# Chunk totals of the log-decays taken from the sum over later tokens and transposed; an odd tile's gate rows taken from the operands of products 3 and 7

## The chip, the cores and the metric

The kernel runs on one core of a Trainium2 chip. The metric is the device time of one execution in microseconds (us), the median of several runs. Engines are named as in the profile: PE is TensorE's matmul pipe (PEld its weight loads), DVE is VectorE, ACT is ScalarE, POOL is GpSimd, SP is SyncE, whose work here is to issue DMAs.

## The reference, cut to what matters

One block of a model: a gated linear attention mixer, then a convolutional feed-forward, each with an RMS norm before it and a residual behind it, and a last norm. The sequence has 2048 tokens, the model 1024 channels, the mixer 4 heads with 128 key and 256 value channels, in chunks of 64 tokens. Only the gate path is touched:

```python
proj = h @ w_in
q, k, v, r, glr = jnp.split(proj, [hk, 2 * hk, 2 * hk + hv, 2 * hk + 2 * hv], axis=-1)   # glr: 16 columns
log_a = jax.nn.log_sigmoid((glr @ w_gate2 + b_gate).astype(jnp.float32)) / GLA_TAU
g = jnp.cumsum(lac, axis=2)            # inside each chunk of 64 tokens
g_end = g[:, :, -1]
k_dec = kc * jnp.exp(g_end[:, :, None] - g)
# per chunk: state = state * exp(g_end) + k_dec^T v;  o = q state
```

So each token needs the exponential of the sum of the log-decays of the tokens that come later in its chunk (it scales the token's key), and each chunk needs the exponential of the whole sum (it scales the state). For the last token of a chunk the first of the two is exp(0) = 1.

## The kernel before, in words

The 2048 tokens are 16 tiles of 128 tokens, two chunks to a tile. The mixer's projections run in four passes over eight pairs of tiles: R (the gate r, and the 16 columns glr), A and B (keys, queries and values of two heads each, with the scan over chunks woven in) and Y (the output projection); the feed-forward follows. Each pass multiplies a pair of tiles (even and odd) with a 1024x1024 block of weights by a seven-product scheme: the left operands are blocks of the pair and their differences, for the odd tile's halves b12 and b22 for instance p5 = b12 - b11, p7 = b22 - b12 and p3 = b22, and for the even tile p1 = b11 and p2 = b21. The order of the products is p1, p5, p6, p7, p4, p2, p3 (PORD). Each is 512 wide and is worked in split single precision: a value is a rounded high part and a rest, and three matmuls make one (`mm3p`, lines 177 to 179, which the profile names mp_R, mp_A and so on; an operand's split is lines 186, ACT, and 187, DVE).

Beside the products of pass R, `gate_mm` makes the gate rows glr of both tiles in one PSUM bank pg: 32 weight columns (the 16, once as high part and once as rest), 128 tokens wide, two matmuls for each of four blocks of 128 channels. The even tile takes p1 and p2. The odd tile takes b11 (p1's operand) plus b12 - b11 (p5's) for the upper half of the channels, and p3's for the lower half, so that p1 is multiplied twice, once for each tile. That is 16 matmuls behind p1 and 8 each behind p5, p2 and p3. After p3, `gate_rows` copies pg into gstk, and after every second pair `gates` works on four tiles: a matmul pz, a softplus (ACT, L555), the split of it in lh and ll (`halves`), and then `sums` for each tile.

`sums` multiplies lh and ll by the mask `later` (L566: 128x128, one where the row token is later than the column token in the same chunk) into the bank pd, takes its exponential (L571, ACT) into es, which a DMA stores (L574). The totals of the two chunks come from eight further matmuls (L570) with lh and ll as weights, one head's 128 channels at a time, and a two-column indicator `chunk` as the moving operand; their exponential (L573, ACT) goes to `dec`, one column for each chunk and head. `scan_f` later loads es again (E) and multiplies the keys by it (L646, kd); the state update (L686) multiplies by dec.

The program is written in one order, with a model clock (`adv`) by which work set aside with `later_do` or in `wevents` is called in between the products. From that order a scheduler at build time makes each engine's order by what it expects to be ready, so the order on an engine is not always that of the program. Each engine then works strictly through its own list.

Of the kernel before, what the change touches and what calls it, by code (L numbers as in the profile page):

```python
# [10 lines left out]
F32 = mybir.dt.float32  # L11
F32R = mybir.dt.float32r
BF16 = mybir.dt.bfloat16
AF = mybir.ActivationFunctionType
ALU = mybir.AluOpType

P = 128
# [3 lines left out]
def f32(ap):  # L21
    return ap.bitcast(F32)
# [3 lines left out]
def hybrid_kernel(  # L26
# [17 lines left out]
    nc = tc.nc  # L44
    x = x[0]
    out = out[0]
# [5 lines left out]
    H, DK, DV, RANK = 4, 128, 256, 16  # L52
    CH = 64
    T = 512
    NT = T // P
    NTT = S // P
    NP = NTT // 2
    KT = D // P
    HK = KT // 2
    NF = F // P  # L60
    QSCALE = float(DK) ** -0.5
    ITAU = 1.0 / 16.0
# [5 lines left out]
    SB = 8  # L68
# [25 lines left out]
    cst = ctx.enter_context(tc.tile_pool(name="cst", bufs=1))  # L94
# [29 lines left out]
    def mm_ps(name):  # L124
        return ps.tile([P, 512], F32, tag="mm", name=name, bufs=4)

    def aux_ps(name):
        return ps.tile([P, 512], F32, tag="aux", name=name, bufs=4)
# [20 lines left out]
    def later_do(us, fn):  # L149
        heapq.heappush(delayed, (clock["now"] + us, next(seq), fn))  # L150

    def adv(us):

        clock["now"] += us
        if clock["busy"]:
            return
        clock["busy"] = True
        for due in (wevents, delayed):
            while due and due[0][0] <= clock["now"]:
                heapq.heappop(due)[-1]()  # L160
        clock["busy"] = False
# [22 lines left out]
    def split(hi, lo, src):  # L184

        nc.scalar.copy(hi, src)  # L186
        nc.vector.tensor_sub(lo, src, f32(hi))  # L187


    ident = cst.tile([P, P], F32, name="ident")  # L190
# [4 lines left out]
    halo = cst.tile([P, 2 * NF, 2], F32, name="halo")  # L195
    dec = cst.tile([P, H, S // CH], F32, name="dec")
    nw2 = cst.tile([P, KT], F32, name="nw2")

    def small(tag, name, n=1, kind=""):
        return cst.tile([P, n], F32, tag=tag + kind, name=name, bufs=4)  # L200
# [164 lines left out]
    rp = {}  # L365
# [75 lines left out]

    def masks():
        rp["later"] = rp["p"].tile([P, P], F32R, name="later")
        rp["chunk"] = rp["p"].tile([P, 2], F32R, name="chunk")

        later_f = rp["p"].tile([P, 512], F32, tag="s2k", name="later_f", bufs=SB)
        nc.gpsimd.memset(later_f[:, :P], 1.0)
        nc.gpsimd.affine_select(
            out=later_f[:, :P], in_=later_f[:, :P], compare_op=ALU.is_gt, fill=0.0,
            base=0, pattern=[[-1, P]], channel_multiplier=1,  # L450
        )
        nc.gpsimd.memset(later_f[CH:P, 0:CH], 0.0)
        nc.vector.tensor_copy(rp["later"], later_f[:, :P])


        ind_f = rp["p"].tile([P, 512], F32, tag="s2k", name="ind_f", bufs=SB)
        nc.gpsimd.memset(ind_f[:, :2], 0.0)
        nc.gpsimd.memset(ind_f[0:CH, 0:1], 1.0)
        nc.gpsimd.memset(ind_f[CH:P, 1:2], 1.0)
        nc.vector.tensor_copy(rp["chunk"], ind_f[:, :2])  # L460

    def gate_weights():

        GR = 2 * RANK
        rp["wg"] = wg = rp["p"].tile([P, 2, KT, GR], F32R, name="wg")
        graw = rp["p"].tile([P, 512], F32, tag="s2k", name="graw", bufs=SB)
        gv = graw[:, :KT * RANK].rearrange("p (a b) -> p a b", b=RANK)
        nc.sync.dma_start(gv, wv[:, :, OR + H * DV:OR + H * DV + RANK])
        nc.gpsimd.memset(f32(wg[:, 1, :, RANK:GR]), 0.0)
        nc.vector.tensor_copy(wg[:, 0, :, :RANK], gv)  # L470
        nc.vector.tensor_copy(wg[:, 1, :, :RANK], gv)
        nc.vector.tensor_sub(wg[:, 0, :, RANK:GR], gv, f32(wg[:, 0, :, :RANK]))

    def gate_weights2():

# [33 lines left out]

    def gate_mm(j, o, hh, hl):  # L510

        if o not in ("p1", "p5", "p2", "p3"):
            return
        GR = 2 * RANK
        if o == "p1":
            rp["pg"] = mm_ps(f"pg_{j}")
        pg = rp["pg"]
        wg = rp["wg"]
        k0 = HK if o in ("p2", "p3") else 0
        for c in {"p1": (0, 1), "p5": (1,), "p2": (0,), "p3": (1,)}[o]:  # L520
            out = pg[:GR, c * P:(c + 1) * P]
            kw = {} if o == "p1" and c == 0 else {"skip_group_check": True}
            for k in range(HK):
                ks = slice(k * P, (k + 1) * P)
                nc.tensor.matmul(out, wg[:, 1, k0 + k, :], hl[:, ks], start=(o == "p1" and c == 0 and k == 0), stop=False, **kw)
                nc.tensor.matmul(out, wg[:, 0, k0 + k, :], hh[:, ks], start=False, stop=(k == HK - 1), **kw)
                adv(0.12)
        if o == "p3":
            gate_rows(j)

# [12 lines left out]
    def gates(b, t0, t1, t2):  # L543

        es, L = [], []

        def s2k(name, dt=F32):
            return rp["p"].tile([P, 512], dt, tag="s2k", name=name, bufs=SB)

        def softplus(half):  # L550
            for tt in (2 * half, 2 * half + 1):
                pz = aux_ps(f"pz_{b}_{tt}")
                nc.tensor.matmul(pz, rp["gstk"][0:98, tt * P:(tt + 1) * P], rp["w2s"][0:98, :], start=True, stop=True)
                e = s2k(f"e_{b}_{tt}")
                nc.scalar.activation(e, pz, AF.Softplus, scale=-1.0)  # L555
                es.append(e)

        def halves(tt):
            lh, ll = s2k(f"lh_{b}_{tt}", F32R), s2k(f"ll_{b}_{tt}", F32R)
            split(lh, ll, es[tt])  # L560
            L.append((lh, ll))

        def sums(tt):
            pd = aux_ps(f"pd_{b}_{tt}")
            for i in range(2):
                nc.tensor.matmul(pd, rp["later"], L[tt][1 - i], start=(i == 0), stop=(i == 1))  # L566
            pe = aux_ps(f"pe_{b}_{tt}")
            for h in range(H):
                for i in range(2):
                    nc.tensor.matmul(pe[:, 2 * h:2 * h + 2], L[tt][1 - i][:, h * DK:(h + 1) * DK], rp["chunk"], start=(i == 0), stop=(i == 1))  # L570
            nc.scalar.activation(es[tt], pd, AF.Exp, scale=-ITAU)  # L571
            t = b * NT + tt
            nc.scalar.activation(dec[:, :, 2 * t:2 * t + 2], pe[:, :2 * H].rearrange("p (a b) -> p a b", b=2), AF.Exp, scale=-ITAU)  # L573
            nc.sync.dma_start(ed[t], es[tt])  # L574
            ready.add(f"gates{t}")
            if tt + 1 < NT:
                later_do(0.4 * t2, lambda: halves(tt + 1))

        later_do(t0, lambda: softplus(0))
        later_do(t0 + 2.0, lambda: softplus(1))  # L580
        later_do(t0 + 4.0, lambda: halves(0))
        for tt in range(NT):
            later_do(t0 + t1 + t2 * tt, lambda tt=tt: sums(tt))
# [51 lines left out]
    def scan_f(n):  # L635
        if n not in scan:
            return
        g, t, kq, e = (scan[n][k] for k in ("g", "t", "kq", "e"))
        if sp.get("gnw_of") != g:
            sp["gnw_of"] = g  # L640
            sp["gnw"] = sp["a"].tile([P, 512], F32, tag="gnw", name=f"gnw_{g}", bufs=1)
            nc.sync.dma_start(sp["gnw"], gla_norm_w[512 * g:512 * (g + 1)].partition_broadcast(P))
        kz = sp["kz"]
        q = sp["q"][t % 2]
        kd = sp["a"].tile([P, 2 * DK], F32, tag="kd", name=f"kd_{n}", bufs=1)
        nc.vector.tensor_mul(kd, kq[:, :2 * DK], e)  # L646
        for c in range(2):
            own = slice(c * CH, (c + 1) * CH)
            split(kz[0][own, c, :], kz[1][own, c, :], kd[own, :])
        pq = aux_ps(f"pq_{n}")  # L650
        for h in range(2):
            nc.tensor.transpose(pq[:, h * P:(h + 1) * P], kq[:, (2 + h) * DK:(3 + h) * DK], ident)
        pv = pq[:, :2 * P].rearrange("p (a c s) -> p a c s", c=2, s=CH)
        for c in range(2):
            sl = (slice(None), slice(None), slice(2 * c * CH, (2 * c + 1) * CH))
            nc.scalar.activation(q[0][sl], pv[:, :, c, :], AF.Copy, scale=QSCALE)
            nc.vector.scalar_tensor_tensor(q[1][sl], pv[:, :, c, :], QSCALE, f32(q[0][sl]), op0=ALU.mult, op1=ALU.subtract)
        r = scan[n]["r"] = sp["a"].tile([P, 512], F32, tag="r", name=f"r_{n}", bufs=2)
        nc.sync.dma_start(r, rd[t][g])
        nc.scalar.activation(r, r, AF.Silu)  # L660
        nc.gpsimd.tensor_mul(r, r, sp["gnw"])
# [230 lines left out]
    def first_pair():  # L892
# [24 lines left out]
        for t in range(2):  # L917
            norm_x(t)
            blocks_x(t)
        masks()  # L920
        nc.gpsimd.memset(halo, 0.0)
        b = {}
# [575 lines left out]
    for n, (o, s) in enumerate(units):  # L1498
# [10 lines left out]
        for q in range(NQ):  # L1509
            k = n * NQ + q  # L1510
# [43 lines left out]
```

## Time and profile before

| | |
|---|---|
| median of 3 runs | 2225.44 us (2217.04 to 2226.3) |
| profiled execution | 2224.22 us, span 2222.5 us |
| PE busy | 2122.4 us, 95% of the span, 9952 matmuls |
| DVE, ACT, POOL busy | 1636.5, 1107.9, 733.1 us |
| granted TensorE clock, mean | 0.986 of full speed |

The span is what the profiler saw from the first to the last instruction; the profiled execution's own time is 1.7 us longer. Busy shares are means over stages that are limited by different things, so a change in pass R (about 53 to 241 us) is read from rows of that stretch.

### The profile page before, as it was taken

Reading aid. Unit: us, or ns where it says so; the run is one execution under the profiler, and the core shown is the slowest. Engines: PE = TensorE matmul, PEld = TensorE weight load, DVE = VectorE, ACT = ScalarE, POOL = GpSimd, SP = SyncE. Lnnn points to the kernel's source line nnn. Section 1 sums busy time; section 2 is a strip of 40 time slices with the busy share of each in tenths; the row PEclk is TensorE's granted clock in tenths of the full one; section 3 lists DMA queues with packets and bytes.
Section 4 is the critical chain, followed back from the end, with each engine's and each line's share of the span. In section 5 each row is a group of like instructions: output and inputs, shape, how many; then the busy total and the mean of one; then the engine's idle time right before and its main releaser. Section 6 shows DMA issues by size and latency. Waiting matters only on the chain.

```text
span 2222.5 us, 29090 instructions
## 1 busy us (share of the span) xinstructions
PE 2122.4 (95%) x9952; PEld 1743.6 (78%) x9952; DVE 1636.5 (74%) x2167; ACT 1107.9 (50%) x2024; POOL 733.1 (33%) x602
## 2 busy tenths in 40 slices
PE   6999999989998999898999999999999999999998
PEld 5888787877887787677887777788888887888886
DVE  8655787789778765488899786897877777457564
ACT  5554755565556676444555453454554443333342
POOL 1000011111111000355566664656555435036100
PEclk9999999999999999999999999999999999999999
DMA  6645684478557889935435348433332468354453
GB/s 210 218 165 182 203 264 157 131 223 299 164 161 235 283 321 352 315 117 174 155 120 193 105 139 288 142 112 102 103 111 85 159 243 289 128 180 152 142 176 113
DMA packets 305125, 411.78 MB, mean 185 GB/s; under 512 B 23742, under 2 KB 160110, under 8 KB 304976
## 3 DMA queue, kind: packets, MB, share of 16 engines
q1 hardware_dynamic: 267440, 346.99, 47.2%
q10 hardware_dynamic: 37536, 62.93, 8.4%
q8 instruction: 78, 1.28, 0.2%
q14 instruction: 71, 0.58, 0.1%
HBM read 266.70 MB, written 143.13 MB: 184 GB/s over the span
## 4 chain that ended last, share of the span: by engine, by line
PE 62%; DVE 14%; DMA 9%; issue 7%; ACT 3%; POOL 3%; SPq 1%; ACTq 0%; DVEq 0%; POOLq 0%
PE ua L177 5%; PE pd_p L178 5%; PE pd_p L179 5%; PE pd_p L177 5%; PE ua L179 5%; PE ua L178 5%; DVE t L1237 4%; PE uc L177 2%; PE uc L179 2%; PE uc L178 2%; PE mp_R L177 2%; PE mp_R L179 2%; PE mp_R L178 2%; PE mp_Y L177 2%; PE mp_Y L179 2%
## 5 line engine op out<-in xcount | busy, mean ns | idle before, releaser
L177 PE MATMUL ua<-h_p,uw_p 128*128 128x512 f32 x704 | 280.2, 398 | 23.6 <-ACT c L1219 23.6
L178 PE MATMUL ua<-h_p,uw_p 128*128 128x512 f32 x704 | 278.6, 396 | 0.0
L179 PE MATMUL ua<-h_p,uw_p 128*128 128x512 f32 x704 | 278.4, 395 | 0.0
L1237 DVE SCALAR_TENSOR_TENSOR t<-u,cw,t 128x1024 f32<-128x1024 f32 x176 | 263.3, 1500 | 8.9 <-ACT t L1235 7.9
L178 PE MATMUL pd_p<-dw_p,da 128*128 128x512 f32 x616 | 240.5, 390 | 3.1 <-DVE da L187 3.1
L179 PE MATMUL pd_p<-dw_p,da 128*128 128x512 f32 x616 | 240.1, 390 | 0.0
L177 PE MATMUL pd_p<-dw_p,da 128*128 128x512 f32 x616 | 240.1, 390 | 0.0
L187 DVE TENSOR_TENSOR uw_p<-ur,uw_p 128x512 fp32r<-128x512 f32 x176 | 168.3, 972 | 58.5 <-ACT uw_p L186 53.3
L187 DVE TENSOR_TENSOR da<-da_p,da 128x512 fp32r<-128x512 f32 x154 | 133.6, 920 | 105.4 <-ACT da L186 105.3
L186 ACT CAST da<-da_p 128x512 fp32r<-128x512 f32 x154 | 85.2, 619 | 208.9 <-PE pd_p L179 153.3
L177 PEld LDWEIGHTS ua<-h_p,uw_p 128*128 128x128 f32 x704 | 134.1, 191 | 57.2 <-ACT c L1219 27.6
L186 ACT CAST uw_p<-us 128x512 fp32r<-128x512 f32 x132 | 82.1, 622 | 165.8 <-POOL us L1199 108.3
L187 DVE TENSOR_TENSOR uw_p<-us,uw_p 128x512 fp32r<-128x512 f32 x132 | 120.4, 921 | 57.6 <-ACT uw_p L186 57.2
L179 PEld LDWEIGHTS ua<-h_p,uw_p 128*128 128x128 f32 x704 | 134.0, 190 | 30.1
L178 PEld LDWEIGHTS ua<-h_p,uw_p 128*128 128x128 f32 x704 | 134.3, 191 | 29.5
L177 PE MATMUL uc<-h_p,uw_p 128*128 128x512 f32 x352 | 138.3, 393 | 1.0 <-DVE t L1237 1.0
L179 PE MATMUL uc<-h_p,uw_p 128*128 128x512 f32 x352 | 138.0, 392 | 0.0
L178 PE MATMUL uc<-h_p,uw_p 128*128 128x512 f32 x352 | 138.0, 392 | 0.0
L178 PEld LDWEIGHTS pd_p<-dw_p,da 128*128 128x128 f32 x616 | 116.0, 188 | 28.0 <-DVE da L187 3.9
L1235 ACT ACTIVATE t<-u,cw 128x1024 f32<-128x1024 f32 x88 | 109.8, 1247 | 51.2 <-DVE u L1328 43.3
L179 PEld LDWEIGHTS pd_p<-dw_p,da 128*128 128x128 f32 x616 | 116.0, 188 | 24.2
L177 PEld LDWEIGHTS pd_p<-dw_p,da 128*128 128x128 f32 x616 | 115.9, 188 | 24.0
(269 smaller groups left out, 5476.2 us busy)
## 6 DMA issues: line engine op xcount, KB each, us to landing
ur<-in_ffn_w_up_dram SPq DMA_DIRECT2D x168, 256.0 KB, 3.7
da_p<-ad_p SPq DMA_DIRECT2D x154, 256.0 KB, 4.1
h_p<-hd_p SPq DMA_DIRECT2D x56, 512.0 KB, 8.1
ad_p<-as_p SPq DMA_DIRECT2D x88, 256.0 KB, 2.7
ad_p<-t SPq DMA_DIRECT2D x66, 256.0 KB, 3.5
x<-in_x_dram SPq DMA_DIRECT2D x32, 512.0 KB, 4.3
ch<-in_ffn_w_down_dram SPq DMA_DIRECT2D x61, 256.0 KB, 4.4
hr_A_p<-h1d_p SPq DMA_DIRECT2D x56, 256.0 KB, 2.7
```

The lines of the kernel that those rows point to most:

```text
L177: nc.tensor.matmul(ps_ap, ah, bl, start=(first and i == 0), stop=False, **kw)
L178: nc.tensor.matmul(ps_ap, al, bh, start=False, stop=False, **kw)
L179: nc.tensor.matmul(ps_ap, ah, bh, start=False, stop=(last and i == len(pairs) - 1), **kw)
L186: nc.scalar.copy(hi, src)
L187: nc.vector.tensor_sub(lo, src, f32(hi))
L1235: nc.scalar.activation(t, u[:, 2:2 + TS], AF.Identity, scale=cw[:, 2, c:c + 1], bias=cw[:, 3, c:c + 1])
L1237: nc.vector.scalar_tensor_tensor(t, u[:, k:k + TS], cw[:, k, c:c + 1], t, op0=ALU.mult, op1=ALU.add)
```

## The change

Two things are changed. In `sums` the mask `later` gets a column of ones over the own chunk for the last token of each chunk, so that rows 63 and 127 of pd hold the chunk totals in place of zero; es is then transposed on PE, head by head, and DVE copies columns 63 and 127 of the result to dec. The eight narrow matmuls, the mask `chunk` and the second exponential go. Since the keys' factor of a chunk's last token must stay 1, `scan_f` takes the maximum of E and `lastrow` (1 in rows 63 and 127, 0 elsewhere) in the same instruction that multiplies the keys. In `gate_mm` the odd tile's gate rows come from p7 = b22 - b12, with the upper half's weights negated, and p3 = b22, with the sum of both halves' weights; the new weights wgx are made once, by DVE and POOL, from work set aside in `gate_weights`. p1 is multiplied once, p5 no longer.

```diff
 def masks():
-        rp["chunk"] = rp["p"].tile([P, 2], F32R, name="chunk")
...
+        nc.gpsimd.memset(later_f[0:CH, CH - 1:CH], 1.0)
+        nc.gpsimd.memset(later_f[CH:P, P - 1:P], 1.0)
         nc.vector.tensor_copy(rp["later"], later_f[:, :P])
-        ind_f = rp["p"].tile([P, 512], F32, tag="s2k", name="ind_f", bufs=SB)
-        nc.gpsimd.memset(ind_f[:, :2], 0.0)
-        nc.gpsimd.memset(ind_f[0:CH, 0:1], 1.0)
-        nc.gpsimd.memset(ind_f[CH:P, 1:2], 1.0)
-        nc.vector.tensor_copy(rp["chunk"], ind_f[:, :2])
+        nc.vector.tensor_add(lastrow, ident[:, CH - 1:CH], ident[:, P - 1:P])
 def gate_weights():
+        rp["wgx"] = wgx = rp["p"].tile([P, 2, KT, GR], F32R, name="wgx")
...
+        nc.gpsimd.memset(f32(wgx[:, 1, :, RANK:GR]), 0.0)
+        def others():
+            gx_ = graw[:, KT * RANK:2 * KT * RANK].rearrange("p (a b) -> p a b", b=RANK)
+            nc.vector.tensor_add(gx_[:, :HK], gv[:, :HK], gv[:, HK:])
+            nc.vector.tensor_scalar(gx_[:, HK:], gv[:, :HK], -1.0, 0.0, op0=ALU.mult, op1=ALU.add)
+            nc.vector.tensor_copy(wgx[:, 0, :, :RANK], gx_)
+            nc.vector.tensor_copy(wgx[:, 1, :, :RANK], gx_)
+            nc.vector.tensor_sub(wgx[:, 0, :, RANK:GR], gx_, f32(wgx[:, 0, :, :RANK]))
+        later_do(24.0, others)
 def gate_mm(j, o, hh, hl):
-        if o not in ("p1", "p5", "p2", "p3"):
+        if o not in ("p1", "p2", "p3", "p7"):
...
-        k0 = HK if o in ("p2", "p3") else 0
-        for c in {"p1": (0, 1), "p5": (1,), "p2": (0,), "p3": (1,)}[o]:
+        c = int(o in ("p3", "p7"))
+        wg = rp["wgx" if c else "wg"]
+        k0 = HK if o in ("p2", "p7") else 0
 def sums(tt):
             for i in range(2):
                 nc.tensor.matmul(pd, rp["later"], L[tt][1 - i], start=(i == 0), stop=(i == 1))
+            nc.scalar.activation(es[tt], pd, AF.Exp, scale=-ITAU)
+            t = b * NT + tt
             pe = aux_ps(f"pe_{b}_{tt}")
             for h in range(H):
-                for i in range(2):
-                    nc.tensor.matmul(pe[:, 2 * h:2 * h + 2], L[tt][1 - i][:, h * DK:(h + 1) * DK], rp["chunk"], start=(i == 0), stop=(i == 1))
-            nc.scalar.activation(es[tt], pd, AF.Exp, scale=-ITAU)
-            t = b * NT + tt
-            nc.scalar.activation(dec[:, :, 2 * t:2 * t + 2], pe[:, :2 * H].rearrange("p (a b) -> p a b", b=2), AF.Exp, scale=-ITAU)
+                nc.tensor.transpose(pe[:, h * DK:(h + 1) * DK], es[tt][:, h * DK:(h + 1) * DK], ident)
+            pv = pe.rearrange("p (h c s) -> p h c s", c=2, s=CH)
+            nc.vector.tensor_copy(dec[:, :, 2 * t:2 * t + 2], pv[:, :, :, CH - 1])
             nc.sync.dma_start(ed[t], es[tt])
 def scan_f(n):
-        nc.vector.tensor_mul(kd, kq[:, :2 * DK], e)
+        nc.vector.scalar_tensor_tensor(kd, e, lastrow, kq[:, :2 * DK], op0=ALU.max, op1=ALU.mult)
```

## Rows read from the trace of the kernel before

**Rows 1.** Stretches: us, PE, PEld, DVE, ACT, POOL busy (instructions), PE clock, DMA share, GB/s.

```profile
50.00:80.00 30.00, 29.93 (x169) 24.46 (x168) 26.02 (x40) 13.97 (x26) 3.52 (x4) 1.00 0.83 291
80.00:110.00 30.00, 29.98 (x180) 24.88 (x179) 17.14 (x27) 18.03 (x33) 1.41 (x2) 1.00 0.47 159
...
290.00:520.00 230.00, 216.78 (x1138) 182.39 (x1137) 190.56 (x351) 131.56 (x299) 33.26 (x33) 0.98 0.62 200
```

**Rows 2.** Waits of PE, 50 to 280 us and whole span: total us, times, longest.

```profile
PE mp_A L177 <- ACT cp_A L1128: 3.9, 1, 3.9
PE mp_R L178 <- DVE h_R_p L187: 0.8, 1, 0.8
...
PE px L718 <- DVE og L710: 8.5, 6, 3.7
```

**Rows 3.** The chain that ended last, pieces between 92 and 111 us: start, us, what.

```profile
93.06 0.87 PE pt_a L397 x8
93.94 0.47 PE pd L566 x2
94.40 0.34 PE mp_R L177
94.74 0.23 PE mp_R L178
...
96.59 0.79 PE pe L570 x8
...
106.97 0.06 PE pg L525
...
107.45 0.28 PE mp_R L177
```

**Rows 4.** DVE and PE instructions by line: ns min/median/max, first and last start.

```profile
L718 PE MATMUL px<-ident,og x128: 270/272/473, 297.6 to 744.6; 128*128 128x128 f32 x128
L472 DVE TENSOR_TENSOR wg<-graw,wg x1: 279/279/279, 16.1 to 16.1; 128x128 fp32r<-128x128 f32 x1
L646 DVE TENSOR_TENSOR kd<-o_A,E x16: 415/418/1556, 268.4 to 475.3; 128x256 f32<-128x256 f32 x16
L686 DVE SCALAR_TENSOR_TENSOR state<-state,dec,pk x128: 465/474/482, 282.4 to 736.3; 128x256 f32<-128x256 f32 x128
```

**Rows 5.** The timeline of ACT around the exponentials of pd: start, us, instruction.

```profile
95.03 0.60 ACT L571 ACTIVATE e<-pd 128x512 f32<-128x512 f32 x1
...
105.42 0.60 ACT L571 ACTIVATE e<-pd 128x512 f32<-128x512 f32 x1 [1.96 <-PE pd L566]
...
268.97 1.28 ACT L571 ACT_TABLE_LOAD   x1
270.27 0.60 ACT L571 ACTIVATE e<-pd 128x512 f32<-128x512 f32 x1
...
275.04 0.60 ACT L571 ACTIVATE e<-pd 128x512 f32<-128x512 f32 x1
```

**Rows 6.** The timeline of PE: the second matmul of pd for the same four tiles.

```profile
94.01 0.40 PE L566 MATMUL pd<-lh,later 128*128 128x512 f32 x1
...
104.99 0.39 PE L566 MATMUL pd<-lh,later 128*128 128x512 f32 x1
...
267.33 0.39 PE L566 MATMUL pd<-lh,later 128*128 128x512 f32 x1
...
274.61 0.39 PE L566 MATMUL pd<-lh,later 128*128 128x512 f32 x1
```

**Rows 7.** The timeline of PE at the first state update of the scan.

```profile
280.24 0.39 PE L680 MATMUL pk<-vl,kz 128*128 128x256 f32 x1 [0.26 <-POOL kz L616]
280.46 0.40 PE L177 MATMUL mp_A<-w_A_p,h_A_p 128*128 128x512 f32 x1
```

**Rows 8.** The timeline of PE after the longest wait at the start of pass A.

```profile
254.57 0.53 PE L177 MATMUL mp_A<-w_A_p,h_A_p 128*128 128x512 f32 x1 [3.86 <-ACT cp_A L1128]
254.91 0.62 PE L178 MATMUL mp_A<-w_A_p,h_A_p 128*128 128x512 f32 x1
```

More of the change, by code (lines that the diff above doesn't have):

```diff
@@ L197, in hybrid_kernel @@
     nw2 = cst.tile([P, KT], F32, name="nw2")
+    lastrow = cst.tile([P, 1], F32, name="lastrow")
     def small(tag, name, n=1, kind=""):
@@ L516, in gate_mm @@
             rp["pg"] = mm_ps(f"pg_{j}")
-        pg = rp["pg"]
-        wg = rp["wg"]
-        k0 = HK if o in ("p2", "p3") else 0
-        for c in {"p1": (0, 1), "p5": (1,), "p2": (0,), "p3": (1,)}[o]:
[L521 to L527, printed above, removed]
+        c = int(o in ("p3", "p7"))
+        wg = rp["wgx" if c else "wg"]
+        k0 = HK if o in ("p2", "p7") else 0
+        out = rp["pg"][:GR, c * P:(c + 1) * P]
+        kw = {} if o == "p1" else {"skip_group_check": True}
+        for k in range(HK):
+            ks = slice(k * P, (k + 1) * P)
+            nc.tensor.matmul(out, wg[:, 1, k0 + k, :], hl[:, ks], start=(o == "p1" and k == 0), stop=False, **kw)
+            nc.tensor.matmul(out, wg[:, 0, k0 + k, :], hh[:, ks], start=False, stop=(k == HK - 1), **kw)
+            adv(0.12)
         if o == "p3":
```

## The prediction

> **What bounds the kernel now.** I read the stretches first. In pass R PE is busy for all but 0.1 us of every 30, while DVE and ACT have 4 to 16 us to spare [rows 1]. The granted clock is 1.00, the upper level of 2.4 GHz. The waits of PE between 50 and 280 us agree: two entries, one of 3.9 us at the start of pass A, one of 0.8 [rows 2]. The chain that ended last, read next, runs on PE through pass R. So from about 53 to 241 us each microsecond taken off PE's list is one off the time, and each one added is one more. At the end of R and in A the chain passes to weight loads, DVE and ACT, but all of that is released by PE's progress in R and moves with it. In A PE works 216.8 of 230 us and DVE 190.6 [rows 1]: there a wait counts in part only.
>
> PE's real price of an instruction is its start to start in the chain, not its busy time, because matmuls overlap. A main product costs 0.23 us. A group of eight chunk-total matmuls costs 0.79 us, a pair of pd 0.47, eight transposes of x 0.87, one gate matmul 0.06. The first product behind narrow work starts dearer: 0.34 in place of 0.23 behind pd, 0.28 behind gate matmuls [rows 3].
>
> **The gate rows.** Seven pairs go through `gate_mm` (the first pair takes `gate_plain`, untouched). Each has 40 matmuls now and 32 afterwards. The number of blocks stays four (p1, p7, p2, p3 for p1, p5, p2, p3), so the dearer first product behind a block is paid as often as now. What goes is 7 x 8 x 0.06 = **-3.4 us** [rows 3]. I see no reason for less or more.
>
> The block behind p5 moves behind p7, two products later. So p5's operand pair comes free 0.5 us earlier and p7's 0.5 us later, and with it ACT's cast for a later operand. PE has waited for such an operand once, for 0.8 us [rows 2], so I take nothing; with that cover gone it would be 7 x 0.5 = 3.4 us. No DMA is added or moved; on SP's queue the store of es has the same place and the same releaser, the exponential.
>
> **The new weights.** Five small DVE instructions of at most 0.28 us each [rows 4], 1.4 us in all, called at 24 us of the model clock, which by the order of the code is the start of the second pair, near 55 us. They are wanted at its p7, some 10 us later. DVE is busy 26.0 of 30 us there and PE does not wait [rows 1, 2]: nothing, or 1.4 us once if they hold up an operand that PE wants. POOL's memsets fall where it is nearly idle (3.5 of 30 us busy [rows 1]): nothing.
>
> **The chunk totals.** Sixteen times, eight narrow matmuls (0.79 us) give way to four transposes. By the transposes of x these cost 0.87 / 2 = 0.44 us [rows 3]: 16 x 0.35 = -5.6 us. But the narrow matmuls mostly stand right behind pd now, so that the dearer next product (0.34 for 0.23) is paid once for both. The transposes wait for the exponential, so products will stand between pd and them, and the 0.11 is paid twice: up to 16 x 0.11 = +1.8 us, about +1.5 since two of the sixteen groups, the one at 96.59 for instance, are apart already [rows 3]. Sum **-4.1 us**.
>
> The Trainium skill speaks against this trade: "TensorE: Matmul & The Clock Gate", Part 4 on PE-mode transpose, gives about 275 ns for one 128x128 transpose in a kernel's context. The busy time of one here is indeed 272 ns [rows 4], but the row of the chain has eight of them in 0.87 us. By the page's figure, taken as start to start, four would be an estimated 1.10 us and the whole trade would lose time; that case is a rival below.
>
> **The new wait.** This is the unknown. Before, the narrow matmuls needed only lh and ll. Now PE needs es, which ACT makes after pd, and every product queued behind the transposes on PE waits with them. From the end of pd's second matmul to the end of the exponential it is 105.42 + 0.60 - 104.99 - 0.39 = 0.64 us where ACT is free, 1.22 us with a table load in front (95.63 - 94.41), and 3.15 us at worst (270.87 - 267.72) [rows 5, 6]. I did this for all 16 tiles (first and last are shown): 22.7 us, of which seven tiles have 0.63 to 0.70 and nine have 1.22 to 3.15, together 18.1.
>
> How much of it PE pays depends on where the transposes stand in its list. That list is not the program's: pk's first matmul is followed by a main product [rows 7], though the program issues pk's six in a row, and at 94.40 nine main products stand between pd and the narrow matmuls that follow it in the code [rows 3]. So the scheduler fills with products (0.23 us each) what it expects to wait. Below: it expects each exponential rightly, and PE pays nothing. Above: it fills 0.66 us for every tile and never expects a table load or a late ACT; the nine long tiles then cost 18.1 - 9 x 0.66 = 12.2 us. Directly behind pd, without filling, would be the full 22.7; that is a rival. Between the ends I go by the nearest row, PE transposes that wait for a value of another engine: px for og, 8.5 us over 128 / 4 = 32 groups, 0.27 us each [rows 2, 4]. Sixteen of them: **+4.3 us**.
>
> What else hangs on it: ACT loses 16 short exponentials and DVE gets 16 copies of eight elements, on engines with room in R [rows 1]. Were a copy late, its bank of the four `aux` ones would come free late; dec itself is wanted only by the scan, after 280 us. Nothing. The masks come before the first sums by some 70 us. Nothing.
>
> **The keys' factor.** 32 instructions of DVE change kind. The median of the multiply is 418 ns, that of the state update, of the new kind and the same size though from PSUM, 474 ns [rows 4]: +0.06 us each, 1.8 us on DVE in A and B. PE does not wait for kd directly there, and DVE is not full; between 0 and 1.8, I take **+0.5 us**.
>
> **Sum.** -3.4 - 4.1 + 4.3 + 0.5 = -2.7 us. The profiled execution took 2224.2 us (span 2222.5 and 1.7 around it), 1.2 us under the median of the three runs. 2224.2 - 2.7 = **2221.5 us**. With the wait at 0 and at 12.2 it is 2217.2 and 2229.4, the likeliest case's own range. I can tell a change from none at about 0.5%, 11 us.
>
> **Rivals.**
>
> *All hidden.* The scheduler places the transposes well and PE pays under 0.1 us a tile: -7.0 us, 2217. For it: PE hardly waits in R, where everything else was placed by the same scheduler. Against it: px.
>
> *The start of pass A is mended as well.* PE waits 3.86 us there for an ACT copy, and the nine products after it start 0.43 apart at half clock (0.62 us long for 0.39 [rows 8]), 1.8 us more. If the freed ACT time and earlier buffers (lh and ll lose their reader on PE) take this wait away too, then -7.0 - 5.7 = -12.7 us, 2211.5. Against it: ACT is late there for weight casts that the change does not touch.
>
> *The transposes stand right behind pd.* Then PE pays the 22.7 us, no dearer product twice (-9.0 in place of -7.5), and behind the longest stalls the clock goes down to 1.2 GHz as it did after 3.86 us, three times 1.8 us: -9.0 + 22.7 + 5.4 + 0.5 = +19.6 us, 2244, slower than before. It decides from a mean stall of 1.2 us a tile on (16 x 1.2 = 19.2, against 9.0 saved). Against it: the filling seen in [rows 3, 7]. For it: nine of sixteen lags are above 1.2 us, and one product is 0.23.
>
> *The transposes do not overlap.* Four take 4 x 0.27 = 1.09 us: the trade gives 16 x 0.30 + 1.5 = +6.3 in place of -4.1, and the time is 2232. Against it stands the row of eight in 0.87 us [rows 3]. The figure of the Trainium skill above would come out this way.
>
> **How the numbers follow.** Forecast 0.50; all hidden 0.20; pass A mended too 0.14; right behind pd 0.12; no overlap 0.04. "Mended" is faster by over 0.5%, and so is, with the spread of measurement, about a fifth of "all hidden" (7 of 11 us): 0.14 + 0.04 = 0.18. "Right behind pd" is slower, with 0.02 from the upper ends of the forecast and of "no overlap": 0.14. The rest, 0.68, lies within. The range 2210 to 2236 holds all but 2244 and the outer half of "mended".
>
> **What would show it.** The lines of the gate matmuls in `gate_mm` count 112 each where they count 140 now. The transposes' four start within 0.44 us. The row to look at first is PE's wait for ACT at them: 0.3 us each bears the forecast out, none the first rival, 1.2 and more the third. Three to five products between pd and them show the filling. The 3.86 us wait of pass A should be there still, some 3 to 7 us earlier. I am wrong if the wait is far from 4 us in sum, or if pass R gains and A or B gives it back because their order was made anew.

## The result and the profile after

The changed kernel takes 2229.64 us (median of 16 runs, 2223.9 to 2234.01), the kernel before 2222.43 us (16 runs, 2216.8 to 2226.88). The ratio is 1.0033, 95% interval [1.0023, 1.0044]: 7 us slower. That is less than the 0.5% which the prediction counts as no change, but it is clear of 1, and on the other side of it than the forecast (-2.7 us). The profiled execution took 2227.88 us, its span is 2225.9.

Where it went is seen from the first start of each pass's products. This is the view of one tile of the kernel after, for the products of R, A and B; the two times are the first and the last start.

```profile
L177 PE MATMUL mp_R<-w_R_p,h_R_p x196: 387/393/736, 55.7 to 247.1; 128*128 128x512 f32 x196
L177 PE MATMUL mp_A<-w_A_p,h_A_p x224: 387/389/794, 248.2 to 467.9; 128*128 128x512 f32 x112
L177 PE MATMUL mp_B<-w_B_p,h_B_p x224: 387/389/628, 468.6 to 703.7; 128*128 128x512 f32 x112
```

Before, the same three first starts were 53.6, 241.2 and 463.8. So the second pair starts 2.0 us later (55.66 for 53.65), pass R is 192.6 us long in place of 187.6 (+5.0), and pass A then takes 220.4 in place of 222.5. A second profile of the same changed kernel has 192.8 for R and 222.6 for A. R repeats to 0.2 us; A and what follows move by 2 to 5 us from one execution to the next, so single profiles are read for the start and for R alone below, and the start only to about 1.5 us (see the start, below).

The waits of PE between 50 and 290 us, after (total us, times, longest), answer to [rows 2]; before there was one of 0.8 in R and the 3.9 of pass A:

```profile
PE pe L580 <- ACT e L576: 5.5, 7, 2.8
PE mp_A L177 <- ACT cp_A L1138: 3.3, 1, 3.3
PE mp_R L177 <- DVE o_R L1082: 2.8, 5, 0.7
PE mp_R L177 <- DVE var_a L208: 1.6, 1, 1.6
PE mp_R L177 <- ACT cp_R L1138: 1.1, 2, 0.5
```

Pass R has 10.9 us of waits in place of 0.8. The first line is the forecast's "new wait". The third to fifth were not forecast. The stretches after (PE, PEld, DVE, ACT, POOL busy; granted clock; DMA share; GB/s) show it too; PE was full in the first of these before [rows 1]:

```profile
80.00:110.00 30.00, 27.94 (x159) 22.65 (x158) 18.08 (x30) 17.36 (x30) 1.09 (x2) 1.00 0.44 164
200.00:230.00 30.00, 26.08 (x143) 21.26 (x142) 18.63 (x30) 13.90 (x24) 0.00 (x0) 0.94 0.71 231
```

**The wait at p4.** Product p4 accumulates in the PSUM bank in which p1, p6 and p7 were summed, and DVE must first have read that bank for o22 (o_R, L1082). The chain that ended last passes from DVE to PE there, after (start, us, what):

```profile
95.22 0.70 DVE o_R L1082
...
95.96 0.50 PE mp_R L177
```

And DVE and PE there, from the timeline (the bracket is the idle time before the instruction and who ended it):

```profile
94.02 1.28 DVE L380 SCALAR_TENSOR_TENSOR x<-x,rstd_a,nw_mix 128x1024 f32<-128x1024 f32 x1 [0.73 <-POOL rstd_a L210]
95.22 0.68 DVE L1082 TENSOR_TENSOR o_R<-mp_R,cp_R 128x512 f32<-128x512 f32 x1
...
95.10 0.22 PE L535 MATMUL pg<-h_R_p,wgx 128*32 128x128 f32 x1
95.96 0.50 PE L177 MATMUL mp_R<-w_R_p,h_R_p 128*128 128x512 f32 x1 [0.64 <-DVE o_R L1082]
...
98.15 1.04 PE L398 MATMUL pt_a<-ident,x 128*128 128x128 f32 x8
```

The same place before, DVE and then PE:

```profile
93.51 0.68 DVE L1072 TENSOR_TENSOR o_R<-mp_R,cp_R 128x512 f32<-128x512 f32 x1
...
94.25 0.49 PE L177 MATMUL mp_R<-w_R_p,h_R_p 128*128 128x512 f32 x1
```

DVE works the norm of a later token tile (x, 1.28 us, itself held by POOL) ahead of o_R. That order is old: before, o_R also stood behind x, at 93.51. But before, eight transposes of x and a pair of pd [rows 3] stood on PE ahead of the next product, and o_R was done at 94.19, just as the product's turn came, at 94.25. After, only two transposes and the eight gate matmuls of p7 stand there, the latter 0.06 us apart, and the eight transposes come at 98.15, inside p4. What stands on PE while it would else wait is called the cover below; most of it is gone. The wait that the view gives to var_a is of the same kind: o_R ends at 151.82 there, p4 starts at 151.88, and var_a is only the instruction behind o_R on DVE. The waits for cp_R are p7's: ACT must first have copied p6's sum out of the same bank. Why the transposes went: up to there a pair has eight gate matmuls fewer, and `gate_mm` moves the model clock by 0.12 for each two matmuls. So at the end of p7 the model clock stands 0.96 us lower than before (eight matmuls of p1 and eight of p5 less), and 0.48 lower behind p7's block, while the transposes are still called at its fixed 10.8 and 13.5 us.

**The wait at the new transposes.** One of the usual kind, from PE's timeline after:

```profile
108.52 0.39 PE L575 MATMUL pd<-lh,later 128*128 128x512 f32 x1
108.75 0.22 PE L534 MATMUL pg<-h_R_p,wgx 128*32 128x128 f32 x1
...
108.93 0.22 PE L535 MATMUL pg<-h_R_p,wgx 128*32 128x128 f32 x1
109.60 0.66 PE L580 MATMUL pe<-ident,e 128*128 128x128 f32 x4 [0.45 <-ACT e L576]
110.01 0.30 PE L534 MATMUL pg<-h_R_p,wgx 128*32 128x128 f32 x1
```

ACT is free there, the exponential starts at 108.95 and lasts 0.60. The scheduler has filled with four gate matmuls, 0.24 us, not with products. Six of the seven waits are of this kind, 0.45 to 0.51 us. At a first tile, where ten matmuls of the products stand between pd and the transposes (at 100.20 to 102.49), there is none. The seventh is this one (PE, then ACT, then DVE, timelines after):

```profile
226.42 1.10 PE L580 MATMUL pe<-ident,e 128*128 128x128 f32 x4 [2.77 <-ACT e L576]
...
228.60 0.63 PE L178 MATMUL mp_R<-w_R_p,h_R_p 128*128 128x512 f32 x1
229.03 0.63 PE L179 MATMUL mp_R<-w_R_p,h_R_p 128*128 128x512 f32 x1
...
225.29 0.36 ACT L547 CAST gstk<-pg 32x256 fp32r<-32x256 f32 x1 [4.06 <-DVE gstk L546]
225.77 0.60 ACT L576 ACTIVATE e<-pd 128x512 f32<-128x512 f32 x1
...
223.51 1.22 DVE L292 TENSOR_TENSOR xsum<-wr_A,wr_A 128x1024 f32<-128x1024 f32 x1 [4.51 <-DMA wr_A<-in_gla_w_in_dram]
...
224.84 0.41 DVE L546 TENSOR_TENSOR gstk<-pg,gstk 32x256 fp32r<-32x256 f32 x1
```

Read from below: DVE's list has a sum of pass A's weights that waits 4.51 us for its DMA; the gate rows' rest (gstk) stands behind it; ACT's next cast waits for that, and the exponential, whose input has long been there, stands behind the cast. Before the change nothing on PE hung on this exponential. Behind the stall the products start 0.43 us apart and the granted clock of the stretch is 0.94.

**The start.** The five DVE instructions of the new weights run early; those that write wgx, after (view of one tile; first and last start behind the durations), and then the stretch from 30 to 40 us (columns as above):

```profile
L478 DVE CAST wgx<-graw x1: 226/226/226, 20.1 to 20.1; 128x128 fp32r<-128x128 f32 x1
L479 DVE CAST wgx<-graw x1: 224/224/224, 35.0 to 35.0; 128x128 fp32r<-128x128 f32 x1
L480 DVE TENSOR_TENSOR wgx<-graw,wgx x1: 292/292/292, 39.7 to 39.7; 128x128 fp32r<-128x128 f32 x1
```

```profile
30.00:40.00 10.00, 10.00 (x51) 8.25 (x50) 10.00 (x12) 3.32 (x4) 0.00 (x0) 1.00 0.01 2
```

DVE is full there: it makes the first pass's weights. Its order has changed too: the first of the sums wr_R started at 39.44 before, ahead of two splits of other weights, and starts at 42.19 behind them now. Behind that sum a weight cast of ACT starts at 43.45 where it was 40.74, and a copy behind that cast at 44.40 where it was 42.17; PE waits for the copy until 45.04 where it was 42.81. How long the first products then take also varies: with all three mends (below) PE goes on at 43.37 and has products 0.23 us apart; the same kernel with another multiply, far behind the start, goes on at 43.42, has them 0.43 apart up to 46.5, and reaches the second pair 1.5 us later.

**As forecast** went what is counted or fixed: the gate matmuls are 112 on each line and 0.06 us apart; the four transposes take 0.41 us from the first start to the next instruction's (109.60 to 110.01); the keys' multiply has a median of 478 ns where it was 418; pass A's opening wait of 3.3 us is still there.

### The profile page after: what moved, and what is told of

Its sections match the earlier page's. It is cut to its first block, busy times and chain, and to the rows that moved or that the text cites. A ratio compares the mean times of both kernels' runs of the same rounds, so it can differ in the third digit from the quotient of the medians.

```text
span 2225.9 us, 28867 instructions
## 1 busy us (share of the span) xinstructions
PE 2106.3 (95%) x9832; PEld 1734.9 (78%) x9832; DVE 1657.9 (74%) x2188; ACT 1106.7 (50%) x2010; POOL 734.8 (33%) x602
## 4 chain that ended last, share of the span: by engine, by line
PE 61%; DVE 16%; DMA 9%; issue 5%; ACT 4%; POOL 3%; SPq 1%; ACTq 0%; DVEq 0%; POOLq 0%
PE pd_p L178 5%; PE pd_p L179 5%; PE pd_p L177 5%; PE ua L177 5%; PE ua L179 5%; PE ua L178 5%; DVE t L1247 4%; PE uc L177 2%; PE uc L179 2%; PE uc L178 2%; PE mp_Y L177 2%; PE mp_Y L179 2%; PE mp_Y L178 2%; DVE uw_p L187 2%; PE mp_R L177 2%
## 5 line engine op out<-in xcount | busy, mean ns | idle before, releaser
L1247 DVE SCALAR_TENSOR_TENSOR t<-u,cw,t 128x1024 f32<-128x1024 f32 x176 | 271.8, 1549 | 7.5 <-ACT t L1245 6.3
L187 DVE TENSOR_TENSOR uw_p<-ur,uw_p 128x512 fp32r<-128x512 f32 x176 | 172.9, 1005 | 49.1 <-ACT uw_p L186 47.5
L178 PEld LDWEIGHTS pd_p<-dw_p,da 128*128 128x128 f32 x616 | 115.6, 188 | 27.8 <-DVE da L187 3.8
L671 POOL TENSOR_TENSOR r<-r,gnw 128x512 f32<-128x512 f32 x32 | 49.3, 1540 | 265.1 <-ACT r L670 216.2
L177 PEld LDWEIGHTS pd_p<-dw_p,da 128*128 128x128 f32 x616 | 115.6, 188 | 25.3 <-DVE u L1320 1.4
```

The costliest lines, as they stand in the source:

```text
L177: nc.tensor.matmul(ps_ap, ah, bl, start=(first and i == 0), stop=False, **kw)
L178: nc.tensor.matmul(ps_ap, al, bh, start=False, stop=False, **kw)
L1247: nc.vector.scalar_tensor_tensor(t, u[:, k:k + TS], cw[:, k, c:c + 1], t, op0=ALU.mult, op1=ALU.add)
```

## The experiments

All are timed in five rounds against the kernel before on the same chip. "Start" is the first product of the second pair, "R" the time from there to the first product of pass A, "waits" PE's idle time in R in gaps of over 0.15 us, all three read from the one profiled execution of each.

| kernel | ratio to before, 95% | start | R | waits in R |
|---|---|---|---|---|
| before | 1 | 53.6 | 187.6 | 0.8 |
| after | 1.0033 [1.0023, 1.0044] | 55.7 | 192.6 | 10.9 |
| after once more | 1.0022 [1.0011, 1.0034] | 55.7 | 192.8 | 11.2 |
| gate rows only | 1.0018 [1.0001, 1.0034] | 53.8 | 191.5 | 8.2 |
| chunk totals only | 1.0001 [0.9983, 1.0018] | 52.2 | 194.3 | 10.1 |
| transposes called later | 1.0007 [0.9987, 1.0028] | 56.4 | 187.7 | 8.3 |
| x transposes called earlier | 0.9987 [0.9970, 1.0003] | 56.7 | 185.1 | 6.0 |
| new weights on POOL | 1.0020 [1.0005, 1.0036] | 52.8 | 197.2 | 13.2 |
| both calls moved | 0.9980 [0.9967, 0.9994] | 55.5 | 180.8 | 3.6 |
| all three mends | 0.9963 [0.9951, 0.9975] | 52.6 | 182.9 | 5.5 |
| before, x transposes earlier | 1.0011 [0.9997, 1.0024] | 53.6 | 189.4 | 2.0 |
| gate rows only, mended | 0.9985 [0.9968, 1.0002] | 52.7 | 186.5 | 4.5 |
| chunk totals only, called later | 0.9993 [0.9981, 1.0006] | 52.1 | 191.7 | 7.4 |
| all three mends, plain multiply | 0.9964 [0.9950, 0.9979] | 54.1 | 182.9 | 4.2 |

**The two halves.** The kernel before with one part of the change each.

Gate rows only: `gate_weights` and `gate_mm` of the change, the rest as before.

```diff
-        if o not in ("p1", "p5", "p2", "p3"):
+        if o not in ("p1", "p2", "p3", "p7"):
...
+        later_do(24.0, others)
```

> The kernel before with only the gate rows of the change (chunk totals by the eight narrow matmuls as before). Pass R, from the first product of its second pair to the first product of pass A, is 187.6 us in the trace before and 192.6 after the whole change. Theory F (filler): the scheduler puts the gate matmuls of p7, 0.06 us each, where products stood between p7 and p4, and p4 waits for DVE's read of the bank they share. Then 3.4 us of matmuls go and about 4 us of waits at p4 come (0.6 us a pair, one longer): R 187 to 189 us, ratio 1.000 to 1.002. Theory T (the totals alone are at fault): no wait at p4 worth naming, R 184 to 185 us, ratio 0.997 to 0.999. Theory D (the maximum on the keys' factor slows DVE in passes A and B): this kernel lacks it, so A and B are as before.

Chunk totals only: `masks`, `sums` and `scan_f` of the change, the rest as before.

```diff
-                    nc.tensor.matmul(pe[:, 2 * h:2 * h + 2], L[tt][1 - i][:, h * DK:(h + 1) * DK], rp["chunk"], start=(i == 0), stop=(i == 1))
+                nc.tensor.transpose(pe[:, h * DK:(h + 1) * DK], es[tt][:, h * DK:(h + 1) * DK], ident)
...
-        nc.vector.tensor_mul(kd, kq[:, :2 * DK], e)
+        nc.vector.scalar_tensor_tensor(kd, e, lastrow, kq[:, :2 * DK], op0=ALU.max, op1=ALU.mult)
```

> The kernel before with only the chunk totals of the change (gate rows from p1 twice, p5, p2 and p3 as before). Theory F: the transposes still stand behind one to four gate matmuls or too few products, PE waits some 5 us for the exponentials in all, against 4 to 5.6 us of matmuls that go: R 186 to 189 us, ratio 0.999 to 1.002, no waits at p4. Theory T: all the loss of the whole change is here, R 191 to 193 us, ratio 1.003. Theory D: R as in F, but passes A and B together 2 us or more longer than the 457.5 us of before.

The gate half, costed at -3.4 us, measured 2227.61 us against 2223.86. PE's waits in its R (same view as above), and then those of the other half:

```profile
PE mp_R L177 <- ACT cp_R L1140: 3.5, 3, 2.4
PE mp_R L177 <- DVE o_R L1084: 3.2, 5, 1.1
PE mp_R L177 <- DVE var_a L207: 1.5, 1, 1.5
```

```profile
PE pe L568 <- ACT e L564: 5.4, 4, 1.8
PE mp_R L178 <- DVE h_R_p L187: 4.7, 1, 4.7
```

Each wait has its owner: those for o_R and var_a, at p4, and those for cp_R, at p6 and p7, come with the gate half alone, those for the exponential with the totals half alone. The totals half has a further one of 4.7 us at the end of R, for an operand; to that below. In both halves R is longer than either theory had it (191.5 and 194.3 us), by the waits for cp_R in the one and the operand's in the other; the ratios lie where theory F had them. Passes A and B are not longer with the maximum in them (451.3 us together, 457.5 before), so theory D is not borne out. The start is not additive: +0.2 us with the gate half, -1.5 with the other half, +2.0 with both.

**Each wait by itself.** Transposes called later: the changed kernel, but the transposes and the copy to dec are called 2 us of the model clock after the exponential.

```diff
+            nc.sync.dma_start(ed[t], es[tt])
+            def totals():
...
+            later_do(2.0, totals)
...
-            nc.sync.dma_start(ed[t], es[tt])
```

> The changed kernel with the transposes and the copy to dec called 2.0 us of the model clock after the rest of the sums, so that six or more main products stand before them in most tiles; nothing else differs. Theory F: the 5.5 us of waits at the transposes go, with the clock fall behind the longest: R 185 to 188 us, 5 to 8 us faster than the change, ratio to before 0.999 to 1.001. Theory D or a cause at the start of the program: R improves by as much but the whole time by less than 2 us, ratio 1.002 to 1.004.

X transposes called earlier: the changed kernel, with one line changed.

```diff
-    TX = (10.8, 13.5)
+    TX = (9.8, 11.8)
```

> The changed kernel with the transposes of the next x tiles called 1.0 and 1.7 us of the model clock earlier in each pair, so that eight of them (0.87 us) stand with p7's gate matmuls between p7 and p4, as they stood before the change; nothing else differs. Theory F: the waits at p4 (five of 0.2 to 0.66 us and one of 1.55 in the trace after) go, 3 to 4 us: R 188 to 190 us, ratio 1.001 to 1.002. If the waits come from DVE being late and not from what stands between p7 and p4, they stay: R 192 to 193 us, ratio 1.003.

PE's waits in R with the later call:

```profile
PE pe L583 <- ACT e L576: 2.8, 1, 2.8
PE mp_R L177 <- DVE o_R L1086: 2.8, 5, 0.7
PE mp_R L177 <- DVE var_a L208: 1.6, 1, 1.6
```

The six short ones are gone, the long one (the exponential behind ACT's cast) has stayed, and p4's waits are untouched; R is 4.9 us shorter. In the whole time this does not show: the interval [0.9987, 1.0028] reaches into that of the changed kernel. With the earlier call of the x transposes:

```profile
PE pe L580 <- ACT e L576: 4.2, 7, 1.6
PE mp_R L177 <- ACT cp_R L1138: 1.1, 2, 0.6
PE mp_R L177 <- DVE var_a L208: 0.7, 1, 0.7
```

The wait for o_R is gone, R is 7.5 us shorter, where 3 to 4 was expected, and the whole time is clear of the changed kernel's (intervals [0.9970, 1.0003] and [1.0023, 1.0044]). Not all of this is p4's: 3.7 us of its waits went, but the long wait at the end of R also fell from 2.77 to 1.60 us, and the granted clock, 0.94 in the changed kernel's stretch from 200 to 230 us, stayed at 1.00. The timeline of PE (then DVE) at the place shown above says why p4 no longer waits:

```profile
95.34 0.22 PE L535 MATMUL pg<-h_R_p,wgx 128*32 128x128 f32 x1
95.40 1.04 PE L398 MATMUL pt_a<-ident,x 128*128 128x128 f32 x8
96.26 0.50 PE L177 MATMUL mp_R<-w_R_p,h_R_p 128*128 128x512 f32 x1
...
95.53 0.68 DVE L1082 TENSOR_TENSOR o_R<-mp_R,cp_R 128x512 f32<-128x512 f32 x1
```

DVE is no earlier than in the changed kernel (95.53 for 95.22). The eight transposes stand between p7's gate matmuls and p4 again, and o_R ends at 96.21 under them. So at p4 it was the cover and not DVE's pace.

**The start, and all together.** The changed kernel once more, then the five DVE instructions of the new weights on GpSimd, then both calls moved, then all three mends.

> The changed kernel once more, unaltered, for a second trace of it. If what the first trace shows is of the program and not of that execution, the first product of the second pair starts again near 55.7 us (53.6 before), the five new DVE instructions again fall between 20 and 40 us, pass R again takes 192 to 193 us, and the waits at the transposes and at p4 stand at the same places. Ratio 1.002 to 1.005.

```diff
         def others():
-            nc.vector.tensor_add(gx_[:, :HK], gv[:, :HK], gv[:, HK:])
+            nc.gpsimd.tensor_add(gx_[:, :HK], gv[:, :HK], gv[:, HK:])
...
```

(and so the other four instructions of `others`)

> The changed kernel with the five instructions that make wgx on POOL in place of DVE; nothing else differs. Theory S (start): DVE is busy throughout from 30 to 45 us, the five cost it 1 us there and push the sum for the third weight block behind the split of another, so that the copy of pt_a and then PE come late; on POOL they cost nothing. Then the second pair starts at 53 to 54 us for 55.7 and the ratio falls by 0.0008 to 0.001, to 1.002 or 1.0025. Rival: the late start is the clock at 1.2 GHz in the first products alone; then it stays at 55 to 56 us.

> The changed kernel with both mends in pass R: the transposes of es called 2.0 us later on the model clock, the transposes of x 1.0 and 1.7 us earlier. Theory F: the two gains add up, R about 180 to 183 us (192.6 after, 187.7 and 185.1 with one mend), and since what R gives stays in part with the weight loads at the start of A, the time is 5 to 10 us under the change: ratio 0.998 to 1.000. If the time after R follows the weight loads alone, R is shorter and A longer by the same, ratio 1.002 to 1.003.

> The changed kernel with all three mends: wgx made on POOL, the transposes of es later, the transposes of x earlier. If the three causes are the whole of the loss, what is left is the saved work, 7.5 us by the forecast's sum: second pair at 53 to 54 us, R 180 to 183 us, ratio 0.996 to 0.998. If something outside pass R and the start also costs (the maximum on the keys' factor, the order of A and B), it stays at 0.999 to 1.001.

The last of the three that write wgx, with the new weights on POOL:

```profile
L480 POOL TENSOR_TENSOR wgx<-graw,wgx x1: 1415/1415/1415, 16.9 to 16.9; 128x128 fp32r<-128x128 f32 x1
```

The new weights are made by 18.3 us, the wait of PE for the copy ends at 43.60 in place of 45.04, and the second pair starts at 52.8 in place of 55.7. Of these 2.8 us (52.85 for 55.66) the earlier copy is 1.4; the rest is the pace behind the wait, 0.43 us a product at first in the changed kernel and 0.23 here. But alone this gave nothing: R grew to 197.2, the waits for the exponential and for o_R rose to 6.2 and 4.0 us, and the granted clock was 0.93 to 0.95 in three of R's seven stretches of 30 us, where the changed kernel has one such. Over all traces with both parts the second pair starts at 52.6 to 54.1 us with the new weights on POOL (three traces) and at 55.5 to 56.7 with them on DVE (five). So the start is a cause shown by its place; its worth in the whole time is not settled, since with the other two mends the step from 0.9980 to 0.9963 is no larger than their intervals, which overlap, and pass A starts only 0.9 us earlier (235.5 for 236.4).

With both calls moved the kernel is faster than before by 0.2%, with all three by 0.37%: 2213.63 us (five runs) against 2221.6. That is 12.6 us below the changed kernel run beside it (2226.25). Both ratios are what was expected. PE's waits in R with all three:

```profile
PE mp_R L177 <- ACT cp_R L1142: 3.0, 3, 2.0
PE mp_R L177 <- DVE var_a L208: 1.7, 2, 1.0
PE pe L583 <- ACT e L576: 0.9, 1, 0.9
```

What is left is mostly p7's wait for ACT's copy, which came with the gate half and which no mend touches.

**Was it the change, or only a better place for the x transposes?**

> The kernel before, with nothing of the change, but with the x transposes called earlier in the pair (9.8 and 11.8 us of the model clock for 10.8 and 13.5). My theory: in the kernel before, the transposes already stand ahead of p4 and PE hardly waits there (0.8 us in pass R), so the earlier call has nothing to mend: ratio to before 1.000, within 0.002. Rival: the earlier call is a tuning of its own that has nothing to do with the change; then this kernel gains what it gained in the changed one, 0.003 to 0.004 (7 to 10 us), and the best version beats the kernel before because of it alone.

The kernel before with the earlier call alone is at 1.0011 [0.9997, 1.0024], R 189.4 us: no gain. The earlier call mends what the change broke and is no tuning of its own.

**What each half is worth when mended.**

> The gate half of the change alone, with the new weights on POOL and the earlier x transposes. My theory: without the wait of p4 and without the later start, the half gives the 3.4 us that 56 fewer gate matmuls are worth: ratio 0.9985 (0.997 to 1.000), and the stretch from the second pair to pass A is 184 us long where it is 187.6 in the kernel before and 191.5 with the half unmended. Rival: the half costs time for another reason (for instance operands that are kept longer): ratio 1.001 and over, stretch 188 and more.

> The other half alone (chunk totals by transposes, gate rows as before), with the transposes called 2 us of the model clock behind the exponential. My theory: the waits for the exponential go, and the half gives the 4.1 us of the cheaper transposes: ratio 0.998 (0.9965 to 0.9995), the stretch from the second pair to pass A 183 to 185 us. Rival: the half stays at no gain (1.000) because the earlier order of the other work is lost, or because passes A and B give it back.

The gate half came to the expected ratio, 0.9985 (2217.43 against 2221.22), though the interval [0.9968, 1.0002] still holds 1, and its R is 186.5 us, not 184: 2.9 us of waits for cp_R and 1.6 at p4 are left in it. The totals half missed: 0.9993, and R is 191.7 us where 183 to 185 was expected. Of its 7.4 us of waits the exponential has 1.4. The rest is mainly one wait; PE's timeline, then DVE's:

```profile
229.53 0.79 PE L178 MATMUL mp_R<-w_R_p,h_R_p 128*128 128x512 f32 x1 [4.77 <-DVE h_R_p L187]
...
231.40 0.63 PE L178 MATMUL mp_R<-w_R_p,h_R_p 128*128 128x512 f32 x1
231.83 0.63 PE L179 MATMUL mp_R<-w_R_p,h_R_p 128*128 128x512 f32 x1
...
226.51 1.22 DVE L296 TENSOR_TENSOR wr_A<-wr_A,wr_A 128x1024 f32<-128x1024 f32 x1 [4.51 <-DMA wr_A<-in_gla_w_in_dram]
...
228.79 0.68 DVE L187 TENSOR_TENSOR h_R_p<-hb,h_R_p 128x512 fp32r<-128x512 f32 x1
```

It is the wait for pass A's weights again, now with PE's operand queued behind it on DVE. Where this wait lands differs from order to order: on the exponential in the changed kernel, on an operand here. Before, the sum that waits 4.51 us in the changed kernel waited 1.84:

```profile
218.83 1.23 DVE L291 TENSOR_TENSOR xsum<-wr_A,wr_A 128x1024 f32<-128x1024 f32 x1 [1.84 <-DMA wr_A<-in_gla_w_in_dram]
```

PE waited for nothing there. In the two kernels without any part of the change this sum waits 1.84 and 1.85 us, in the twelve traces of kernels with a part or all of it 2.1 to 5.7. The reason was not looked for.

**The keys' factor.** All three mends, with the multiply as it was (so the last token's factor of 1 is left out):

```diff
-        nc.vector.scalar_tensor_tensor(kd, e, lastrow, kq[:, :2 * DK], op0=ALU.max, op1=ALU.mult)
+        nc.vector.tensor_mul(kd, kq[:, :2 * DK], e)
```

> All three mends, but the keys' factor is a plain multiply again: the maximum with lastrow is left out, so the last token of each chunk has its key scaled by the chunk total. My theory: the 32 dearer instructions of DVE (0.06 us each) cost under 0.5 us, so this kernel is at the time of the one with all three mends, 0.996 of the kernel before, and passes A and B together have the same length within their spread of 4 us. Rival: the dearer instruction is on the path of the scan, 1.8 us or more: ratio 0.995 or less.

0.9964 [0.9950, 0.9979], with the maximum 0.9963: no difference, but the interval is 6 us wide and holds both 0.5 and 1.8 us. Passes A and B together take 461.4 us, with the maximum 458.0. The term is small; its size stays open.

## Why the prediction was wrong in sign, point by point

**The gate rows: the step that failed.** "What goes is 7 x 8 x 0.06" was right as work. Wrong was "I see no reason for less or more", and that the block moved behind p7 costs nothing ("I take nothing"). I looked for who gets an operand later, and not at what stands on PE just ahead of p4 and what that covers. In p7's place the block is only 0.5 us long, and with eight gate matmuls fewer the call of the x transposes, by a fixed time of the model clock, slipped past p4. The waits at p4, 4.4 us together (2.8 + 1.6), took more than the 3.4, and p7's for ACT's copy came on top (1.1). It was visible before: at 93.06 in [rows 3] stand the eight transposes that are the cover, and o_R ended only 0.06 us before the product that needs it, the same distance as in the waits after, so the cover was just long enough. That this half turned the sign shows in its own run: -3.4 us forecast, 2227.61 for 2223.86 us measured (+3.8, ratio [1.0001, 1.0034]). The other half, -4.1 + 4.3 + 0.5 = +0.7 in the forecast, measured 2223.68 for 2223.86, no change within 4 us.

**The new weights: failed in place.** I took the call at 24 us of the model clock for 55 us of the trace. They ran at 20 to 40 us, where DVE was full (10.00 of 10), and the second pair started 2.0 us later with both halves in; on POOL it started early again, without a gain in the whole time that could be shown.

**The new wait: right mechanism, size 5.5 us of idle for 4.3.** The guess that the scheduler fills was right, the filler was not: where only gate matmuls are at hand it fills with 0.24 us. That six waits agree to 0.06 us fits a steady lag of the exponential (0.6 us) and too short a filler. Seven tiles of sixteen wait, not all at 0.27. The upper tail that the forecast priced, a late ACT, came once (2.77 us), and through a wait of DVE for the next pass's weights, for which the forecast, with no DMA added or moved, had no term. That the total lies near 4.3 is partly luck: the forecast spread px's waits over all tiles, and half of the total is that one wait. It lies where the reading of the stretches was too even: from 200 to 230 us PE was busy 29.08 of 30 us before, not all but 0.1.

**A wait costs more than its idle time.** The forecast's likeliest case added idle times. At 109.60 the transposes start 0.67 us after the last gate matmul, whose own pitch is 0.06: 0.61 us lost, where the row shows 0.45 idle. The rest is the overlap with the instruction before (0.22 us long at 0.06 pitch), and 15 such waits are some 2.4 us, an estimate from this one row. The later call of the transposes points the same way: it took away 2.6 us of idle time, and R fell by 4.9. Behind the longest wait the clock comes on top: a granted clock of 0.94 over 30 us is an estimated 1.8 us.

**The chunk totals: -4.1 forecast, more measured.** Without waits R would be 187.6 - 0.8 = 186.8 us before and 182.9 - 5.5 = 177.4 with all three mends: 9.4 us of PE's work saved in R by both parts, where 7.5 was the forecast with R's tiles and A's. By the time from each PE start to the next in R, less idle time, the gate matmuls fell from 16.8 to 13.6 us (3.2, forecast 3.4), the chunk totals of R's 12 tiles from 9.7 to 4.4 (0.44 a tile, forecast 0.35), and the main products did not get dearer (140.5 and 139.3), where the forecast added 1.5 for them. So the saving was there, and the kernel after lost it: -9.4 + 10.1 of idle time + 2.4 + 1.8 (the two estimates above) = +4.9, measured 192.6 - 187.6 = +5.0. The version with all mends has a few waits of its own, so that the sum closes this well is partly luck. The rival "transposes do not overlap" is out. The figure of the Trainium skill ("TensorE: Matmul & The Clock Gate", Part 4, about 275 ns for one transpose in a kernel's context) agrees with the busy time of one here, median 273 ns, but not as a pitch, the time from one start to the next: four take 0.43 to 0.49 us in the chain, and the measurement decides.

**The other rivals.** "Right behind pd" (2244) did not come: nine of the sixteen tiles wait for nothing. "Pass A mended too" did not come: that wait is there with 3.3 us, also with all three mends. "All hidden" is nearest to what the version with all mends shows: 8 us under the kernel before, where the rival had 7.

**The sum.** Against the 2222.43 us of the same runs the measured change is +7.2 us, in the traces +3.4 (span) to +4.8 (start of pass B). The start (+2.0) and R (+5.0) make +7.0 at the start of pass A. How much of it A and later passes give back can't be read, since they vary by 2 to 5 us between executions. The two halves alone add up to +3.6 us, with intervals some 4 us to either side, so whether the change costs more than its halves stays open.

## What to carry to other kernels

Before narrow work is taken out of an in-order list or moved in it, look at what it covers: for each product next to the edit, who must have finished with its bank or operand, when that ends, and what stands between. Work called at fixed times of a model clock slips when the instructions that move the clock change; call it again after such an edit. When a new dependence on another engine is put into PE's list, look at everything that engine has queued in front, weight loads for the next pass included, and place the dependent work late by call rather than trust that the filler is long enough.

## What the runs showed of the hardware that was not expected

A stall of 2.77 us on PE is followed by products 0.43 us apart (granted clock of the stretch 0.94), one of 4.77 us by the same pitch, while one of 2.05 us with all three mends stands in a stretch with a granted clock of 1.00. GpSimd took 1.42 us for the small subtraction of wgx that takes DVE 0.29, and it did not matter: the weights were made by 18.3 us and first used at 65.8.
